# Positional terms of a block compression taken out of the data and added behind its first layer

## The chip, the cores and the metric

The kernel runs on one core of one Trainium2 chip. The metric is the device time of one execution in microseconds (us). The kernel before takes 863.8 us (median of three runs, 863.54 to 864.02).

## The reference, cut to what matters

One decoder layer over 512 tokens of width 1024: a norm and one wide input projection, two attention mixers (a sparse one called NSA with 8 heads in 2 groups, and a block one called MoBA with 8 heads), a gated merge with an output projection, a feed-forward block of width 2816, and a gated side input. The change touches one corner of NSA, the compression of keys and values. Every 32 neighbouring tokens (in steps of 16) become one flat row of 2048 numbers, a learned positional table `pe` is added, and a two-layer network makes one compressed key or value of 64 numbers from it:

```python
def compress_blocks(t, pe, w1, w2):
    b, g, sp, d = t.shape
    n_sub, per = sp // CMP_STRIDE, CMP_LEN // CMP_STRIDE      # 32 sub-blocks, 2 per block
    sub = t.reshape(b, g, n_sub, CMP_STRIDE, d)
    nc = n_sub - per + 1                                      # 31 blocks
    blocks = jnp.concatenate([sub[:, :, i:i + nc] for i in range(per)], axis=3)
    flat = (blocks + pe).reshape(b, g, nc, CMP_LEN * d)
    return jax.nn.silu(flat @ w1) @ w2

# in nsa_mixer
kc = rms_norm(compress_blocks(to_heads(kc_in, G), pe_k, ck_w1, ck_w2), kc_gain)
vc = compress_blocks(to_heads(vc_in, G), pe_v, cv_w1, cv_w2)
cmp_end = cmp_start + CMP_LEN - 1
s_c = jnp.einsum('bgrtd,bgcd->bgrtc', q, kc) * ATTN_SCALE
p_c = masked_softmax(s_c, cmp_end[None, :] <= t_idx[:, None])
o_c = jnp.einsum('bgrtc,bgcd->bgrtd', p_c.astype(vc.dtype), vc)
```

There are 31 blocks for each of the two groups. With two groups of 32 columns, columns 31 and 63 stand for no block; the mask takes them out of the softmax.

## The kernel before, in words

**Split products.** All large products are made in three passes of a rounded type (`F32R`): a number x is split into a high part h (a ScalarE copy that rounds) and a low part l = x - h (a VectorE subtraction), and TensorE adds h*h, h*l and l*h. This holds for the weights too. Every weight unit is loaded as `wr` (three buffers, issued on SP), split on ScalarE into `wh` (L84) and on VectorE into `wl` (L85), again with three buffers each. A raw buffer comes free, and its next load can start, when L85 has read it; a `wh` or `wl` buffer comes free when TensorE has used it.

**The stage in question.** The input projection of the MoBA queries (`qm`) comes first. Then come the compression's keys and values (`kvc`, tiles `kT` and `vT`, transposed: feature by token), the MoBA keys (`km`, four weight units) with the keys' first compression layer between them (`k1`, four units, in function `hidden`), then `cb`, `qn` with the values' first layer (`v1`), `cc`, `vm`, and after that attention, the gates, the output projection, the feed-forward block and the side input. Units are taken in the order km0, k1_0, km1, k1_1, km2, k1_2, km3, k1_3.

**`compress_in`** (L506 to L532), once for keys and once for values, evacuates the projected tile from PSUM with a factor (`kct`, L510), adds the positional table into a rearranged tile `x32` with eight additions of 64 partitions by 248 numbers (L520, half of them on VectorE, half on GpSimd; the source is read with a step of 16 numbers), and splits the result into high and low halves (L529 on ScalarE, L530 on VectorE, two 128x512 pieces each). These are the stationary operands of `hidden` (L580): one pass of 16 products with `wh` and 16 with `wl`, whose output rows 0 to 63 belong to the high part and rows 64 to 127 to the low one. `hidden` adds the two (L591, L593) and applies SiLU as z*(1+tanh(z/2)) (L594, L595), the factor one half being left to later. `cmp_kv` (L610) turns the 64x256 result with two TensorE transposes (L614), splits it (L617, L618), makes the second layer (L623, L624) and goes on to the compressed keys or values.

**Beside it** run the last steps of the `qm` heads: a rotation on GpSimd (L411 to L414), a split on ScalarE and VectorE (L419, L420, tile `qmst`), TensorE transposes (L439, tile `tb`) and their evictions on ScalarE (L446, tile `QM`).

**Order.** The kernel is written as interleaved generators, and a planner then orders the instructions of each engine: by the order of the program, among those that are ready in its own simulated time. Each engine runs its queue strictly in that order. Small work tiles (`t2`, 128x512) have five buffers, PSUM banks come in pairs by tag; `kT` and `vT` hold the two banks of tag `s`, which `km` needs for its first two token blocks.

Of the kernel before, what the change touches and what calls it, by code (L numbers as in the profile page):

```python
# [10 lines left out]
F32 = mybir.dt.float32  # L11
F32R = mybir.dt.float32r
I32 = mybir.dt.int32
AF = mybir.ActivationFunctionType
OP = mybir.AluOpType
# [7 lines left out]
DH = 64  # L23
# [143 lines left out]
def hybrid_kernel(ctx: ExitStack, tc: tile.TileContext, a, out):  # L167
    nc = tc.nc
    cp = ctx.enter_context(tc.tile_pool(name="cp", bufs=1))
# [5 lines left out]
    V, A, G, T = nc.vector, nc.scalar, nc.gpsimd, nc.tensor  # L175
# [13 lines left out]
    def t5(name, dt=F32):  # L189
        return pp.tile([128, 1280], dt, name=name, tag="t5")  # L190
# [75 lines left out]
    for tt in range(QT):  # L266
# [2 lines left out]

    hg = cp.tile([128, 6, DH], F32, name="hg")  # L270
    nc.sync.dma_start(hg, a["hg"].rearrange("(o h) d -> o h d", o=1).broadcast_to([128, 6, DH]))
    pe = cp.tile([128, 2, 2, 16], F32, name="pe")
    nc.sync.dma_start(pe, a["pe"])

    ident = cp.tile([128, 128], F32, name="ident")
    make_identity(nc, ident)
    identr = cp.tile([128, 128], F32R, name="identr")
    V.tensor_copy(identr, ident)
    half_neg = cp.tile([128, 32], F32, name="half_neg")
    V.memset(half_neg, -0.5)  # L280
    big_mask = cp.tile([128, 512], F32, name="big_mask")
# [2 lines left out]
                    channel_multiplier=1, compare_op=OP.is_ge, fill=BIG)  # L284
# [217 lines left out]
    qm_t, rest = norm_heads("qm", qm_b, None, q_tables[4])  # L502

    XX = {}

    def compress_in(i, nm):  # L506
        o = bank(nm + "T", "s")
        yield from ttile(("kvc", i), o)
        kt_ = t2("kct")
        V.scalar_tensor_tensor(kt_, o, 2.0, rb0, op0=OP.mult, op1=OP.mult)  # L510
        x32 = t5("x32")
        xv = x32[:, :1024].rearrange("p (j c) -> p j c", j=16)
        G.memset(xv[:, :, 31::32], 0.0)
        for g in range(2):
            gs = slice(64 * g, 64 * g + 64)
            kv = kt_[gs].rearrange("p (c j s) -> p s j c", s=2, j=8)
            for s in range(2):
                for hf in range(2):
                    eng = V if (g * 4 + s * 2 + hf) % 2 else G
                    eng.tensor_tensor(xv[64 * s:64 * s + 64, 8 * hf:8 * hf + 8, 32 * g:32 * g + 31],  # L520
                                      kv[:, s, :, hf:hf + 31],
                                      pe[gs, i, s, 8 * hf:8 * hf + 8].unsqueeze(2).to_broadcast([64, 8, 31]),
                                      op=OP.add)
        XX[nm] = []
        for hf in range(2):
            t = flat(t4(f"{nm}xx{hf}"))
            f = t.rearrange("p (j e c) -> p j e c", j=8, e=2)
            x = xv[:, 8 * hf:8 * hf + 8]
            A.activation(f[:, :, 0, :], x, AF.Copy)  # L529
            V.tensor_sub(f[:, :, 1, :], x, f[:, :, 0, :].bitcast(F32))  # L530
            XX[nm].append(t.rearrange("p (j c) -> p j c", j=8))
        yield  # L532

# [46 lines left out]
    def hidden(nm, tag):  # L580
# [10 lines left out]
        A.activation(tmp, o[64:128, :CH], AF.Copy)  # L591
        z = small("hz_", [64, CH])
        V.tensor_tensor(z, o[0:64, :CH], tmp, op=OP.add)  # L593
        A.activation(tmp, z, AF.Tanh, scale=0.5)  # L594
        V.scalar_tensor_tensor(z, tmp, 1.0, z, op0=OP.add, op1=OP.mult)  # L595
        hid[nm] = z

    KC = cp.tile([128, 2, 64], F32R, name="KC")
# [11 lines left out]
    def cmp_kv(i, nm, tag):  # L610
        b = bank(nm + "t2", tag)
        z = hid.pop(nm)
        for m in range(2):
            T.transpose(b[:, m * 64:(m + 1) * 64], z[:, m * 128:(m + 1) * 128], ident[0:64, 0:64])  # L614
        hs = MI[:, 512 + 256 * i:768 + 256 * i].rearrange("p (m e c) -> p m e c", m=2, e=2)
        bv = b[:, :128].rearrange("p (m c) -> p m c", m=2)
        A.activation(hs[:, :, 0, :], bv, AF.Copy, scale=0.5)  # L617
        V.scalar_tensor_tensor(hs[:, :, 1, :], bv, 0.5, hs[:, :, 0, :].bitcast(F32), op0=OP.mult, op1=OP.subtract)  # L618
        yield
# [430 lines left out]
def layout(i):  # L1050
# [20 lines left out]
    pos5 = np.concatenate([pos.reshape(QT, 128).T, np.tile(pos[cend], 4)[:, None]], axis=1)  # L1071

    def pet(p):
        t = p[0].reshape(16, 2, DH).transpose(2, 1, 0)
        return np.concatenate([t, t], axis=0)

    return dict(
        xT=f(i["x"][0].T.reshape(KT, 128, S)),
# [42 lines left out]
```

## Time and profile before

| | us |
|---|---|
| median of three runs | 863.8 |
| profiled execution, its own time | 863.29 |
| its span, first to last instruction | 861.4 |
| TensorE busy with products | 843.4 |
| VectorE busy | 532.2 |
| ScalarE busy | 391.3 |
| GpSimd busy | 139.2 |

The own time is the span and 1.9 us around it. Products overlap in the array, so TensorE shows as busy for a little longer than it issues; a stall costs the distance from one product's start to the next, less the usual distance. Times in the timelines are from the start of the span. A bracket at the end of a row is the engine's idle time ahead of that row and what ended it.

### The profile page before, as it was taken

The numbers are of one execution on the slowest core, as the hardware profiler recorded it, in microseconds if no ns is written. First come the engines' busy times: TensorE is split into PE (matmuls) and PEld (weight loads), VectorE is DVE, ScalarE is ACT, GpSimd is POOL, SyncE is SP. The second block draws the span as 40 slices with busy tenths as digits, with TensorE's granted clock in tenths as the row PEclk, the third lists the DMA queues.
The fourth block names the chain that finished last, engine by engine and source line by source line (L and its number), as shares of the span: only waits on it lengthen the run. The fifth ranks groups of instructions, "written<-read, shape, count | busy, mean of one in ns | idle before, by whom it ended". The sixth has DMA issues, their size and how long they took to land.

```text
span 861.4 us, 11012 instructions
## 1 busy us (share of the span) xinstructions
PE 843.4 (98%) x4169; PEld 708.5 (82%) x4169; DVE 532.2 (62%) x944; ACT 391.3 (45%) x708; POOL 139.2 (16%) x140
## 2 busy tenths in 40 slices
PE   9999999999999999999999999999999999999997
PEld 7878798888788888787888888888888888888886
DVE  6777766878976988749536555555555433233354
ACT  6455545877776877634423222233333222233421
POOL 2735443000000000024321111111111101010100
PEclk9999999999999999999999999999999999999999
DMA  9433525423211111116323333333323333333221
GB/s 328 153 99 98 162 73 142 129 64 89 84 49 50 50 49 36 63 49 216 102 76 121 98 98 97 99 98 97 95 91 94 84 109 87 93 110 97 98 99 49
DMA packets 26996, 85.58 MB, mean 99 GB/s; under 512 B 3392, under 2 KB 3904, under 8 KB 26944
## 3 DMA queue, kind: packets, MB, share of 16 engines
q1 hardware_dynamic: 26016, 82.78, 30.3%
q10 hardware_dynamic: 928, 2.11, 1.0%
q8 instruction: 32, 0.52, 0.3%
q14 instruction: 20, 0.16, 0.1%
HBM read 79.64 MB, written 2.10 MB: 95 GB/s over the span
## 4 chain that ended last, share of the span: by engine, by line
PE 84%; DVE 8%; ACT 2%; POOL 2%; DMA 2%; issue 1%; SPq 0%; DVEq 0%; ACTq 0%; POOLq 0%
PE fg L361 5%; PE fu L362 5%; PE fg L362 5%; PE fob L361 5%; PE fob L362 5%; PE fu L361 5%; PE fg L363 5%; PE fu L363 5%; PE fob L363 5%; PE ga L361 3%; PE ga L362 3%; PE ga L363 3%; PE pt L818 3%; DVE wl L85 2%; PE pgb L361 2%; PE pv L842 2%
## 5 line engine op out<-in xcount | busy, mean ns | idle before, releaser
L84 ACT ACTIVATE wh<-wr 128x1024 fp32r<-128x1024 f32 (+2 forms) x145 | 147.4, 1019 | 310.3 <-PE fu L362 73.6
L85 DVE TENSOR_TENSOR wl<-wr,wh 128x1024 fp32r<-128x1024 f32 (+2 forms) x145 | 196.2, 1357 | 106.0 <-ACT wh L84 105.4
L361 PE MATMUL fg<-x2h,wh 128*128 128x512 f32 x176 | 68.6, 390 | 0.0
L361 PE MATMUL fu<-x2h,wh 128*128 128x512 f32 x176 | 68.6, 390 | 0.0
L363 PE MATMUL fg<-x2h,wl 128*128 128x512 f32 x176 | 68.5, 389 | 0.0
L363 PE MATMUL fu<-x2h,wl 128*128 128x512 f32 x176 | 68.5, 389 | 0.0
L363 PE MATMUL fob<-HH,wl 128*128 128x512 f32 x176 | 68.5, 389 | 0.0
L362 PE MATMUL fu<-x2l,wh 128*128 128x512 f32 x176 | 68.5, 389 | 0.0
L362 PE MATMUL fg<-x2l,wh 128*128 128x512 f32 x176 | 68.5, 389 | 0.0
L362 PE MATMUL fob<-HL,wh 128*128 128x512 f32 x176 | 68.5, 389 | 0.0
L361 PE MATMUL fob<-HH,wh 128*128 128x512 f32 x176 | 68.5, 389 | 0.0
L1008 POOL TENSOR_TENSOR u<-zg,u 128x512 f32<-128x512 f32 x22 | 29.8, 1352 | 199.9 <-DVE u L1006 191.4
L361 PE MATMUL ga<-xh,wh 128*128 128x512 f32 x128 | 53.6, 419 | 0.0
L362 PE MATMUL ga<-xl,wh 128*128 128x512 f32 x128 | 50.3, 393 | 0.0
L363 PE MATMUL ga<-xh,wl 128*128 128x512 f32 x128 | 50.2, 393 | 0.0
L793 DVE CUSTOM_DVE_ANT_0 p<-sb,big_mask 128x512 f32<-128x512 f32 (+2 forms) x96 | 44.9, 484 | 7.3 <-PE sb L791 7.1
L1006 DVE SCALAR_TENSOR_TENSOR u<-fu,rb 128x512 f32<-128x512 f32 x22 | 15.2, 690 | 53.6 <-PE fu L363 53.6
L944 POOL TENSOR_TENSOR GT<-GT,GT 128x512 f32<-128x512 f32 x8 | 14.7, 1856 | 190.5 <-DVE GT L943 190.5
L245 POOL TENSOR_TENSOR ssum<-ssum,sqx 128x512 f32<-128x512 f32 x14 | 22.1, 1575 | 139.1 <-ACT sqx L244 139.1
L818 PE MATMUL pt<-ident,p 128*128 128x128 f32 x240 | 38.2, 274 | 2.8 <-DVE pw L828 2.7
L828 DVE TENSOR_TENSOR pw<-pt,pw 128x512 fp32r<-128x512 f32 x48 | 32.6, 684 | 10.7 <-ACT pw L827 10.3
L361 PEld LDWEIGHTS fu<-x2h,wh 128*128 128x128 f32 x176 | 33.1, 188 | 6.9
(590 smaller groups left out, 1993.5 us busy)
## 6 DMA issues: line engine op xcount, KB each, us to landing
wr<-fi SPq DMA_DIRECT2D x44, 512.0 KB, 3.4
wr<-ga SPq DMA_DIRECT2D x16, 512.0 KB, 3.5
wr<-fo SPq DMA_DIRECT2D x16, 512.0 KB, 3.5
wr<-wo SPq DMA_DIRECT2D x8, 512.0 KB, 3.6
wr<-pg SPq DMA_DIRECT2D x8, 512.0 KB, 3.4
wr<-fo SPq DMA_DIRECT2D x8, 384.0 KB, 3.2
xin<-xT SPq DMA_DIRECT2D x8, 256.0 KB, 5.5
xn<-xN SPq DMA_DIRECT2D x4, 512.0 KB, 7.8
```

The costliest lines, as they stand in the source:

```text
L84: self.nc.scalar.activation(h[:, a:b], t[:, a:b], AF.Copy)
L85: self.nc.vector.tensor_sub(l[:, a:b], t[:, a:b], h[:, a:b].bitcast(F32))
L245: G.tensor_tensor(ssum, ssum, q, op=OP.add)
L361: T.matmul(o, wh[:, sl], h, start=start, stop=False)
L362: T.matmul(o, wh[:, sl], l, start=False, stop=False)
L363: T.matmul(o, wl[:, sl], h, start=False, stop=stop)
L793: V.tensor_tensor_reduce(out=p, in0=o, in1=big_mask[:, 512 - n:512], op0=OP.add, op1=OP.min, scale=1.0, scalar=3.0e38, accum_out=st["m"][: ...
L818: last = T.transpose(b[:, off:off + 128], st["p"][:, P_OFF[qt] + kb * 128:P_OFF[qt] + kb * 128 + 128], ident)
L828: V.tensor_sub(pl, b[:, :off], ph.bitcast(F32))
L842: T.matmul(o, job["v"](kb), st.pop(("pl", kb))[:, cols], start=False, stop=job["last"] and kb == 2)
L1006: V.scalar_tensor_tensor(u, bu, 2.0, rb1, op0=OP.mult, op1=OP.mult)
L1008: G.tensor_tensor(u, zg, u, op=OP.mult)
```

## The change

The positional terms are no longer added to every block. The low-level layout of the table `pe` is changed so that it has the same rows as the rearranged operand, it is split once (`pes`), and its 16 columns for keys or values are put as one more block into the unused columns 31 and 63. The tile of projected keys (or values) is split before it is rearranged, once, and the high and low parts are then placed by copies: the high part on ScalarE, the low part on GpSimd. The first layer is linear, so the row of column 31 behind it is the positional contribution alone. It is added to all rows by the turn in `cmp_kv`: the two transposes become two products with `pos_sum`, an identity matrix whose row 31 is all ones. The nonlinearity has to come after this addition, so tanh and its multiplication move from `hidden` to `cmp_kv`, behind the turn.

```diff
-    pe = cp.tile([128, 2, 2, 16], F32, name="pe")
+    pe = cp.tile([128, 2, 16], F32, name="pe")
     nc.sync.dma_start(pe, a["pe"])
...
+    pos_sum = cp.tile([64, 64], F32, name="pos_sum")
+    V.tensor_copy(pos_sum, ident[0:64, 0:64])
+    G.affine_select(pos_sum, pos_sum, pattern=[[0, 64]], base=-31, channel_multiplier=1,
+                    compare_op=OP.not_equal, fill=1.0)
...
     XX = {}
+    pes = cp.tile([128, 2, 2, 16], F32R, name="pes")
+    A.activation(pes[:, 0], pe, AF.Copy)
+    V.tensor_sub(pes[:, 1], pe, pes[:, 0].bitcast(F32))
 
     def compress_in(i, nm):
         o = bank(nm + "T", "s")
         yield from ttile(("kvc", i), o)
         kt_ = t2("kct")
         V.scalar_tensor_tensor(kt_, o, 2.0, rb0, op0=OP.mult, op1=OP.mult)
-        x32 = t5("x32")
-        xv = x32[:, :1024].rearrange("p (j c) -> p j c", j=16)
-        G.memset(xv[:, :, 31::32], 0.0)
-        for g in range(2):
-            gs = slice(64 * g, 64 * g + 64)
-            kv = kt_[gs].rearrange("p (c j s) -> p s j c", s=2, j=8)
-            for s in range(2):
-                for hf in range(2):
-                    eng = V if (g * 4 + s * 2 + hf) % 2 else G
-                    eng.tensor_tensor(xv[64 * s:64 * s + 64, 8 * hf:8 * hf + 8, 32 * g:32 * g + 31],
-                                      kv[:, s, :, hf:hf + 31],
-                                      pe[gs, i, s, 8 * hf:8 * hf + 8].unsqueeze(2).to_broadcast([64, 8, 31]),
-                                      op=OP.add)
+        kh, kl = t2("kch", F32R), t2("kcl", F32R)
+        A.activation(kh, kt_, AF.Copy)
+        V.tensor_sub(kl, kt_, kh.bitcast(F32))
         XX[nm] = []
         for hf in range(2):
             t = flat(t4(f"{nm}xx{hf}"))
             f = t.rearrange("p (j e c) -> p j e c", j=8, e=2)
-            x = xv[:, 8 * hf:8 * hf + 8]
-            A.activation(f[:, :, 0, :], x, AF.Copy)
-            V.tensor_sub(f[:, :, 1, :], x, f[:, :, 0, :].bitcast(F32))
+            for e, src in ((0, kh), (1, kl)):
+                for g in range(2):
+                    kv = src[64 * g:64 * g + 64].bitcast(F32).rearrange("p (c j s) -> p s j c", s=2, j=8)
+                    for sh in range(2):
+                        o = f[64 * sh:64 * sh + 64, :, e, 32 * g:32 * g + 31]
+                        if e == 0:
+                            A.activation(o, kv[:, sh, :, hf:hf + 31], AF.Copy)
+                        else:
+                            G.tensor_copy(o, kv[:, sh, :, hf:hf + 31])
+                for c in (31, 63):
+                    G.tensor_copy(f[:, :, e, c:c + 1], pes[:, e, i, 8 * hf:8 * hf + 8].bitcast(F32).unsqueeze(2))
             XX[nm].append(t.rearrange("p (j c) -> p j c", j=8))
         yield
...
         V.tensor_tensor(z, o[0:64, :CH], tmp, op=OP.add)
-        A.activation(tmp, z, AF.Tanh, scale=0.5)
-        V.scalar_tensor_tensor(z, tmp, 1.0, z, op0=OP.add, op1=OP.mult)
         hid[nm] = z
...
         for m in range(2):
-            T.transpose(b[:, m * 64:(m + 1) * 64], z[:, m * 128:(m + 1) * 128], ident[0:64, 0:64])
+            T.matmul(b[:, m * 64:(m + 1) * 64], z[:, m * 128:(m + 1) * 128], pos_sum, start=True, stop=True)
+        th = t2("cth")[:, :128]
+        A.activation(th, b[:, :128], AF.Tanh, scale=0.5)
+        V.scalar_tensor_tensor(th, th, 1.0, b[:, :128], op0=OP.add, op1=OP.mult)
         hs = MI[:, 512 + 256 * i:768 + 256 * i].rearrange("p (m e c) -> p m e c", m=2, e=2)
-        bv = b[:, :128].rearrange("p (m c) -> p m c", m=2)
+        bv = th.rearrange("p (m c) -> p m c", m=2)
...
     def pet(p):
-        t = p[0].reshape(16, 2, DH).transpose(2, 1, 0)
-        return np.concatenate([t, t], axis=0)
+        return p[0].reshape(16, 2, DH).transpose(1, 2, 0).reshape(128, 16)
```

## Rows read from the trace of the kernel before

**Rows 1.** The page, part 1: busy us of TensorE, share, instructions.
```profile
PE 843.4 (98%) x4169; PEld 708.5 (82%) x4169; DVE 532.2 (62%) x944; ACT 391.3 (45%) x708; POOL 139.2 (16%) x140
```

**Rows 2.** Windows: stretch, its us, busy us of each engine, clock, DMA.
```profile
40.00:57.00 17.00, 14.86 (x79) 11.88 (x78) 16.46 (x21) 9.22 (x15) 10.64 (x12) 1.00 0.11 34
80.00:93.00 13.00, 9.83 (x58) 7.95 (x56) 11.14 (x12) 5.14 (x12) 10.94 (x9) 1.00 0.48 161
93.00:170.00 77.00, 75.80 (x443) 65.26 (x442) 54.48 (x117) 46.32 (x105) 21.65 (x25) 1.00 0.38 112
```

**Rows 3.** Timeline of TensorE, 44 to 57 us: start, us, what, [idle before].
```profile
44.30 0.94 PE L351 MATMUL km<-wh,xh 128*128 128x512 f32 x3
46.09 0.70 PE L439 MATMUL tb<-identr,qmst 128*128 128x128 f32 x6 [0.86 <-DVE qmst L420]
...
52.27 0.39 PE L351 MATMUL km<-wh,xh 128*128 128x512 f32 x1
52.49 0.39 PE L352 MATMUL km<-wl,xh 128*128 128x512 f32 x1
53.51 0.39 PE L586 MATMUL khid<-wh,kxx 128*128 128x256 f32 x1 [0.63 <-DVE kxx L530]
...
55.45 0.35 PE L586 MATMUL khid<-wh,kxx 128*128 128x256 f32 x1
56.45 0.39 PE L587 MATMUL khid<-wl,kxx 128*128 128x256 f32 x1 [0.65 <-DVE wl L85]
```

**Rows 4.** Timeline of VectorE, 41 to 59 us.
```profile
41.41 3.53 DVE L520 TENSOR_TENSOR x<-kct,pe 64x248 f32<-64x248 f32 x4
44.97 1.07 DVE L420 TENSOR_TENSOR qmst<-qme,qmst 128x512 fp32r<-128x512 f32 x1
...
47.69 3.83 DVE L520 TENSOR_TENSOR x<-kct,pe 64x248 f32<-64x248 f32 x4
...
52.77 1.29 DVE L530 TENSOR_TENSOR kxx<-x,kxx 128x512 fp32r<-128x512 f32 x2
...
55.18 3.58 DVE L85 TENSOR_TENSOR wl<-wr,wh 128x1024 fp32r<-128x1024 f32 x3
```

**Rows 5.** Timeline of ScalarE, 40 to 54 us.
```profile
40.92 1.05 ACT L84 ACTIVATE wh<-wr 128x1024 fp32r<-128x1024 f32 x1
46.67 1.16 ACT L419 ACTIVATE qmst<-qme 128x512 fp32r<-128x512 f32 x2 [4.71 <-POOL qme L414]
...
51.18 1.15 ACT L529 ACTIVATE vxx<-x 128x512 fp32r<-128x512 f32 x2 [2.32 <-POOL x L520]
52.24 1.06 ACT L446 ACTIVATE QM<-tb 128x512 fp32r<-128x512 f32 x2
53.20 1.06 ACT L84 ACTIVATE wh<-wr 128x1024 fp32r<-128x1024 f32 x1
```

**Rows 6.** Groups by line, shapes apart: count, busy us, mean ns, idle before.
```profile
L594 ACT ACTIVATE ht<-hz__1202 64x256 f32<-64x256 f32 x1 | 0.4, 404 | 0.0
L593 DVE TENSOR_TENSOR hz__775<-khid,ht 64x256 f32<-64x256 f32 x1 | 0.4, 408 | 0.0
L318 POOL COPY cs<-cs 128x40 f32<-128x40 f32 x1 | 0.2, 216 | 0.0
L594 ACT ACT_TABLE_LOAD x1 | 1.3, 1283 | 0.0
```

**Rows 7.** Timeline of GpSimd, 41 to 46 us.
```profile
41.77 3.71 POOL L520 TENSOR_TENSOR x<-kct,pe 64x248 f32<-64x248 f32 x4
45.56 1.08 POOL L414 TENSOR_TENSOR qme<-rope 128x256 f32<-128x256 f32 x1
```

**Rows 8.** The chain of work that ended last: start, us, engine, what.
```profile
106.27 0.27 PE kt L614 x2
457.15 0.89 PE st1c L336 x8
```

**Rows 9.** Timelines of ScalarE and TensorE, 102 to 112 us.
```profile
106.57 0.28 ACT L617 ACTIVATE MI<-kt 128x128 fp32r<-128x128 f32 x1 [2.97 <-PE kt L614]
...
111.20 0.27 PE L623 MATMUL ko<-MI 128*128 128x64 f32 x1
```

## The prediction

> **What bounds the kernel now.** I read the page's busy times first, then the windows by stage, then the timelines of the four engines in the one stage that the change touches.
>
> TensorE is busy for 843.4 us of a span of 861.4 [rows 1], so at most 18 us are to be had anywhere without taking products away, and the change takes none away. What matters is how much of that idle time lies where the compression runs. The windows [rows 2] answer it: from 40 to 57 us TensorE is busy for 14.86 of 17.00, and VectorE for 16.46 of 17.00. In this short stage VectorE is the bound and TensorE waits for it. From 93 to 170 us TensorE misses only 1.2 us.
>
> The timeline of TensorE [rows 3] shows three waits there, each ended by VectorE: for `qmst`, for `kxx`, for a `wl`. The usual distance between two products of 512 columns is 0.22 to 0.23 us (52.27 to 52.49), half of that for 256 columns. Against that, 44.30 to 46.09 holds three products (0.68) and loses 1.11 us; 52.49 to 53.51 loses 0.79; 55.45 to 56.45 loses 0.88. Together 2.8 us. Without them the product at 56.45 could start at 53.65.
>
> The timeline of VectorE [rows 4] shows why. Four additions of the positional terms hold it for 3.53 us from 41.41, and the subtraction for `qmst` follows only at 44.97; four more take 3.83 us from 47.69; then come four subtractions of the split (two pairs of 1.29) and only at 55.18 the weight's low part that TensorE wants at 56.45. ScalarE [rows 5] is held up behind this as well: it stands 2.32 us ahead of 51.18, waiting in order for the GpSimd additions of the values, and so rounds the weight k1_1 only at 53.20.
>
> **The change, part by part.**
>
> *VectorE.* Eight additions go: 3.53 + 3.83 = 7.4 us [rows 4]. Four 128x512 subtractions become two: at 1.29 a pair, 1.3 us less. What it gains is a 128x32 subtraction in the set-up, a copy of 64x64, and nothing else in this stage. So 8.7 us of 16.46 go, and VectorE is no longer the bound between 40 and 57 us. The subtraction for `qmst` at 44.97 moves ahead of 44.30, and the first stall goes. What is late next is ScalarE.
>
> *ScalarE.* Four roundings of 128x512 become two (1.15 us a pair [rows 5]); sixteen copies of 64x248 are added. The trace has no ScalarE copy with such a step between elements. From below, the nearest is the 64x256 activation at 0.404 us [rows 6], which read its source without a step; from above, a row of the same shape and step is the addition on VectorE, 3.53/4 = 0.88 us [rows 4], a different engine that shared its time with GpSimd. I take 0.40, the row of the same engine; both ends go into the range. Its queue after the rounding that ends at 41.97 [rows 5]: two roundings 1.15, sixteen copies 16c, the `qmst` pair 1.16, the `QM` pair 1.06, then k1_1's rounding 1.06. Copies of the values are not needed before 93 us, but stand ahead of k1_1 in the program, so I count all sixteen. The rounding ends at 41.97 + 4.43 + 16c = 46.4 + 16c, the subtraction for `wl` takes 1.2 us more (3.58 for three [rows 4]), and with 0.1 for the two hand-overs TensorE gets it at 47.7 + 16c. With c = 0.40 that is 54.1, against 56.45 before and 53.65 at the least: 2.35 us are won, 0.45 of the stalls stay. It breaks even at c = (56.45 - 47.7)/16 = 0.547.
>
> *GpSimd.* Eight additions go, 3.71 us for the first four [rows 7], and sixteen copies of 64x248 with sixteen of 128x8 come. From below, the copy of 128x40 takes 0.216 [rows 6]; from above, the addition took 3.71/4 = 0.93 [rows 7]. I take 0.6, between them, as a copy reads one operand and the additions waited for VectorE. TensorE needs first only the first half (4 large, 2 small for the low part, 2 small for the high part): from about 42.5, with the rotation of 1.08 ahead [rows 7], 42.5 + 1.08 + 4x0.6 + 4x0.2 = 46.8 at my value and 48.1 at the upper one. TensorE has km0 and km1 to do until about 51. So this is hidden, unless the order is unlucky (a rival below). The values' copies have until 93 us.
>
> VectorE's additions took 0.88 each beside GpSimd's and a 64x256 one alone takes 0.408 [rows 4, 6]. [...]
>
> *The turn and the nonlinearity.* In `hidden` a tanh (0.404) and a multiplication (0.41) leave, both beside `cb` products; nothing on TensorE waits. In `cmp_kv` a tanh and a multiplication of 128x128, some 0.3 each like the rounding of that shape (0.28 [rows 9]), enter between turn and second layer, with two hand-overs about 0.9 us. TensorE takes up the result only at 111.20, 4.6 us after ScalarE began at 106.57 [rows 9], so it is covered; without that cover it costs 0.9, twice. The table load of 1.28 us [rows 6] moves with the first tanh; ScalarE stands idle for 2.97 us ahead of 106.57 [rows 9], and the load does not wait for the turn, so it is covered; uncovered it costs 1.28. In ScalarE's queue behind the new tanh stand weight roundings; they are delayed by a third of a microsecond at most.
>
> *TensorE.* Four transposes become four full-precision products. Two transposes take 0.27, four 128x128 full-precision products 0.89 (eight records) [rows 8]: 0.13 against at most 0.22 each. That is 0 to 0.4 us in all, on the bounding engine; I take 0.2.
>
> *Set-up.* The split of `pe`, the 64x64 copy and selection: four small instructions before 40 us, where TensorE does not wait; nothing to 0.2 us. The load of `pe` stays one DMA on SP, smaller; weight loads keep their order and come earlier with the splits that free their buffers.
>
> **Sum.** 863.29 (span 861.4 and 1.9 around it) - 2.35 + 0.2 = 861.1 for a profiled execution. That execution lies 0.5 under the median of 863.8, so for the median 861.65, given as 861.6.
>
> **The rivals.**
>
> *The placing copies on ScalarE are dear (slower).* If a step of 16 numbers between elements costs ScalarE what it costs elsewhere, c is above 0.547 and k1_1 comes later than before. At c = 0.62 TensorE gets it at 57.6: 1.2 later, with 0.2 for the turn 865.2 by the median. At 0.76, not quite the upper end, at 59.9 and 867.4. For it: the additions with this step took twice a plain one; against it: they shared their time with GpSimd's, which alone would explain it. 0.14. [...]
>
> *The first layer is planned too early (no change).* The planner places `khid` as soon as it thinks `kxx` ready. If it believes the GpSimd copies to be quick, the products of k1_0 stand right behind km0, about 45.6, and TensorE waits in order until the low parts are there, 46.8 to 48.1 as worked out, say 1.4 later. Then 0.95 is won, less 0.2: 863.05. For it: the wait at 53.51 is already one for `kxx`; against it: TensorE had most of km1 done by then. 0.17.
>
> *The gain is given back between 57 and 93 us (no change).* From 80 to 93 us TensorE is busy for 9.83 of 13.00 [rows 2], waiting for weight splits on a VectorE that runs beside GpSimd. If those waits hang on something that does not move with TensorE, they grow by what was won: 863.8, or 864.0 with the turn. Against it: the chain there starts from the last `km` product, which moves too. 0.14.
>
> *More goes than I count.* If also some of the waits from 80 to 93 go, another 1 to 2 us: about 860. 0.05.
>
> **How the numbers follow.** The forecast has 0.50, with its own range 861.0 to 862.5 (from c = 0.372, where all 2.8 are won and the turn costs nothing, to c = 0.45). What this kernel can tell from no change is 0.2%, 1.7 us, so faster means below 862.1. About 0.42 of the forecast's 0.50 lies there, and the 0.05 of the last case: 0.47 faster. The other 0.08 of the forecast, the 0.17 of the second rival and 0.12 of the third: 0.37 same. The 0.14 of the first rival, and 0.02 of the third, where the waits grow by more than was won: 0.16 slower. The range for 8 in 10 reaches from 859.8 to 865.2, the upper end being c = 0.62.
>
> **What would show it.** In the changed profile between 40 and 57 us: VectorE busy for about 8 us instead of 16.5, TensorE missing under 1 us instead of 2.1, ScalarE busy for some 14. ScalarE's 64x248 copies at 0.40 and not 0.55; k1_1's `wh` beginning at 51 to 52 instead of 53.2. The table load at about 102 with nothing behind it. The forecast is wrong if `khid` waits for GpSimd, if ScalarE's copies are over 0.55, or if TensorE's idle time from 57 to 170 us grows.

## The result, and the profile after

The changed kernel takes 869.65 us (median of 6 runs, 868.57 to 870.69) against 863.83 us (6 runs, 862.30 to 866.51): a ratio of 1.0063, 95% interval 1.0049 to 1.0076. It is slower by 5.8 us, where 861.6 was forecast, and lies 4.45 us above the upper end of the range. Its profiled execution took 869.96 us, with a span of 868.1; that of the kernel before took 863.29, so the two profiles differ by 6.7 us.

The busy times, page part 1, against [rows 1]:

```profile
PE 848.4 (98%) x4173; PEld 712.6 (82%) x4173; DVE 524.4 (60%) x936; ACT 401.2 (46%) x723; POOL 146.4 (17%) x163
```

VectorE lost 7.8 us, as meant, and ScalarE gained 9.9. But TensorE, which has four products in place of four transposes and nothing else new, is busy for 5.0 us more. Such a figure cannot come from added work; it says that TensorE ran slower somewhere. The windows show where. Columns as in [rows 2]: stretch, its length, busy us of TensorE, of its weight loads, of VectorE, ScalarE, GpSimd, then the granted clock.

```profile
40.00:57.00 17.00, 13.91 (x71) 11.51 (x70) 8.28 (x9) 16.00 (x26) 16.27 (x35) 0.94 0.13 42
57.00:70.00 13.00, 12.46 (x55) 10.14 (x55) 4.97 (x4) 6.25 (x10) 2.09 (x3) 0.68 0.36 121
85.50:98.50 13.00, 9.84 (x58) 7.96 (x56) 11.14 (x13) 5.12 (x12) 10.94 (x9) 1.00 0.49 161
```

VectorE falls from 16.46 to 8.28 in the first stretch, which is the 8 us of the forecast. ScalarE stands at 16.00 of 17.00, and GpSimd, which got copies too, at 16.27; for which of them TensorE waits, the timelines tell. Behind this stretch, from 57 to 70, the granted clock is 0.68. The third line is the stretch of the second line of [rows 2], 5.5 us later: it has the same busy times.

The timeline of ScalarE, 44 to 59 us (start, busy us, what, and in brackets the idle time ahead of it), against [rows 5]:

```profile
43.34 1.16 ACT L423 ACTIVATE qmst<-qme 128x512 fp32r<-128x512 f32 x2 [0.52 <-POOL qme L418]
44.40 5.21 ACT L531 ACTIVATE kxx<-kch 64x248 fp32r<-64x248 f32 x8
49.63 0.63 ACT L519 ACTIVATE kch<-kct 128x512 fp32r<-128x512 f32 x1
50.30 5.14 ACT L531 ACTIVATE vxx<-kch 64x248 fp32r<-64x248 f32 x8
55.46 1.08 ACT L450 ACTIVATE QM<-tb 128x512 fp32r<-128x512 f32 x2
56.57 2.00 ACT L84 ACTIVATE wh<-wr 128x1024 fp32r<-128x1024 f32 x2
```

The sixteen placing copies (now L531) take 10.35 us, 0.65 each. Up to 59 us ScalarE is never idle again. The evictions of `QM` begin at 55.46, where they began at 52.24 before, and the weight of k1_1 is rounded from 56.57, where it was 53.20.

TensorE in the same time, against [rows 3]:

```profile
50.98 0.28 PE L591 MATMUL khid<-wh,kxx 128*128 128x256 f32 x1
...
52.63 0.40 PE L355 MATMUL km<-wh,xh 128*128 128x512 f32 x1
56.12 0.75 PE L443 MATMUL tb<-identr,qmst 128*128 128x128 f32 x4 [3.09 <-ACT QM L450]
...
59.19 0.58 PE L592 MATMUL khid<-wl,kxx 128*128 128x256 f32 x1 [0.54 <-DVE wl L85]
...
64.01 0.63 PE L355 MATMUL km<-wh,xh 128*128 128x512 f32 x1
64.43 0.63 PE L356 MATMUL km<-wl,xh 128*128 128x512 f32 x1
...
65.77 0.39 PE L355 MATMUL km<-wh,xh 128*128 128x512 f32 x1
66.00 0.40 PE L356 MATMUL km<-wl,xh 128*128 128x512 f32 x1
```

The wait for `kxx` at 53.51 of before is gone: `khid` starts at 50.98, and the wait ahead of `tb` at 46.09 is gone too. In their place stands one wait of 3.09 us for an eviction, and a shorter one for the weight. Then look at the distance between two products of 512 columns: 0.42 us at 64.01, and 0.23 again at 65.77. The windows of 2 us give the clock for it:

```profile
54.00:56.00 2.00, 0.00 (x0) 0.00 (x0) 0.00 (x0) 1.95 (x5) 1.85 (x4) 0.76 0.00 0
56.00:58.00 2.00, 1.89 (x10) 1.59 (x10) 0.34 (x1) 1.98 (x4) 1.87 (x4) 0.50 0.00 0
58.00:60.00 2.00, 1.46 (x7) 1.16 (x6) 2.00 (x2) 2.00 (x4) 1.13 (x2) 0.50 0.00 0
...
66.00:68.00 2.00, 2.00 (x13) 1.66 (x12) 0.00 (x0) 0.36 (x1) 0.00 (x0) 1.00 0.30 114
```

TensorE stood still from about 53 to 56.12. In that time its granted clock fell from 1.00 to 0.50, and it came back at about 65.3. At a granted clock of 0.50 a product of 512 columns takes 0.42 us in place of 0.23, which is where most of the 5.0 us of busy time come from.

The chain of waits from 54 to 61 us names the links in order: the last copies, the eviction, the rounding, the subtraction, the product.

```profile
54.81 0.63 ACT vxx L531
...
55.46 1.08 ACT QM L450 x2
...
56.57 1.06 ACT wh L84
...
57.66 1.49 DVE wl L85
...
59.19 0.58 PE khid L592
```

The turn, against the first line of [rows 8] (two transposes, next product 0.26 us after the first started, at 106.46 in that trace):

```profile
111.72 0.66 PE L617 MATMUL kt<-pos_sum,hz__811 64*128 64x64 f32 x4
112.31 0.53 PE L443 MATMUL tb<-identr,kmst 128*128 128x128 f32 x4
```

It takes 0.59 now, 0.33 more, and the other one the same.

### The profile page after: what moved, and what is told of

It reads as the page before. It is cut to its first block, busy times and chain, and to the rows that moved or that the text cites. A ratio compares the mean times of both kernels' runs of the same rounds, so it can differ in the third digit from the quotient of the medians.

```text
span 868.1 us, 11046 instructions
## 1 busy us (share of the span) xinstructions
PE 848.4 (98%) x4173; PEld 712.6 (82%) x4173; DVE 524.4 (60%) x936; ACT 401.2 (46%) x723; POOL 146.4 (17%) x163
## 4 chain that ended last, share of the span: by engine, by line
PE 85%; DVE 6%; ACT 2%; DMA 2%; POOL 2%; issue 1%; SPq 0%; DVEq 0%; POOLq 0%
PE fg L365 5%; PE fu L365 5%; PE fob L367 5%; PE fg L367 5%; PE fu L367 5%; PE fob L366 5%; PE fob L365 5%; PE fu L366 5%; PE fg L366 5%; PE ga L365 3%; PE ga L366 3%; PE ga L367 3%; PE pt L824 3%; DVE wl L85 2%; PE pgb L365 2%; PE pv L848 2%
## 5 line engine op out<-in xcount | busy, mean ns | idle before, releaser
L1014 POOL TENSOR_TENSOR u<-zg,u 128x512 f32<-128x512 f32 x22 | 29.8, 1353 | 199.9 <-DVE u L1012 191.4
L367 PE MATMUL ga<-xh,wl 128*128 128x512 f32 x128 | 50.2, 394 | 0.0
L367 PEld LDWEIGHTS fu<-x2h,wl 128*128 128x128 f32 x176 | 33.1, 188 | 6.9
```

Source lines behind the costliest of these rows:

```text
L367: T.matmul(o, wl[:, sl], h, start=False, stop=stop)
L1014: G.tensor_tensor(u, zg, u, op=OP.mult)
```

## The experiments

Each ratio is to the kernel before as timed beside that kernel, whose median there lay between 863.3 and 864.1; it is taken over all runs and can differ a little from the ratio of the two medians. The other columns are marks on TensorE's timeline in the profiles, us: the end of the wait in the `cb` products that stands at 81.97 before, and the first products of the first turn, of the scores `sb` and of the output projection `uno`.

| kernel | end of that wait | first turn | first `sb` | first `uno` | median, ratio to before [95%] |
|---|---|---|---|---|---|
| before | 81.97 | 106.20 | 156.43 | 366.6 | 863.83 |
| after | 87.50 | 111.72 | 163.03 | 373.1 | 869.65, 1.0063 [1.0049, 1.0076] |
| e1_plain | 80.36 | 104.6 | 155.9 | 365.9 | 863.08, 0.9994 [0.9985, 1.0003] |
| e2_later | 78.89 | 103.10 | 154.4 | 364.5 | 862.33, 0.9977 [0.9967, 0.9986] |
| e3_turn | 82.00 | 106.21 | 157.6 | 369.0 | 865.62, 1.0013 [1.0003, 1.0023] |
| e4_filled | 84.45 | 108.7 | 160.1 | 371.6 | 868.39, 1.0052 [1.0039, 1.0065] |
| e5_vector | 83.46 | 107.7 | 159.1 | 369.1 | 866.91, 1.0031 [1.0019, 1.0043] |
| e6_values_later | 80.71 | 104.9 | 155.2 | 365.4 | 863.35, 0.9990 [0.9980, 0.9999] |
| e7_plain_more | 84.45 | 108.7 | 160.0 | 370.0 | 867.58, 1.0040 [1.0026, 1.0054] |
| e9_later_turned | 78.67 | 102.92 | 153.9 | 364.8 | 861.58, 0.9982 [0.9974, 0.9991] |
| e10_reordered | 80.20 | 104.4 | 155.8 | 367.4 | 863.57, 1.0001 [0.9993, 1.0010] |
| e11_all | 78.90 | 103.1 | 154.1 | 365.0 | 861.66, 0.9981 [0.9972, 0.9990] |

The theory: ScalarE's copies are dear because their source steps by 16 numbers; by their time in ScalarE's queue they hold the evictions and the weight back; the wait that results lowers the clock; and the turn costs besides. The rivals: that number or place of the copies matters and not the step; that the clock falls for another reason; that the turn is most of it.

**e1_plain: the step taken away.** The ScalarE copies read 248 neighbouring numbers: as many, but not in the order that the result needs.

```diff
-    A.activation(o, kv[:, sh, :, hf:hf + 31], AF.Copy)
+    A.activation(o, src[64 * g:64 * g + 64, 0:248].bitcast(F32).rearrange("p (j c) -> p j c", j=8), AF.Copy)
```

> The changed kernel, but ScalarE's placing copies read 248 neighbouring numbers instead of every 16th (as many numbers, the same instructions and destinations; so the high parts are placed in a wrong order). Theory, the step between the numbers makes these copies dear: they take about 0.40 us instead of 0.65, the sixteen end 4 us sooner (about 51.5), the QM evictions behind them come before TensorE asks for their bank at 52.9, the 3.1 us wait and the half clock behind it go, total 861.5 to 863. Rival, it is the number of instructions on ScalarE and not the step: 0.65 us each, total 869.6.

863.08 us, 6.6 under the changed kernel (6.0 by the two ratios). The copies take 0.42 us, and the `QM` evictions begin at 51.20:

```profile
43.75 3.37 ACT L531 ACTIVATE kxx<-kch 64x248 fp32r<-64x248 f32 x8
...
47.81 3.37 ACT L531 ACTIVATE vxx<-kch 64x248 fp32r<-64x248 f32 x8
51.20 1.09 ACT L450 ACTIVATE QM<-tb 128x512 fp32r<-128x512 f32 x2
```

One wait is left between 50 and 60 us, for the weight's low part:

```profile
54.79 0.39 PE L592 MATMUL khid<-wl,kxx 128*128 128x256 f32 x1 [0.98 <-DVE wl L85]
```

Products of 512 columns stay 0.23 us apart behind it (59.55 to 59.78), and the granted clock of the whole profile is 0.999. So one number, 0.65 against 0.42, decides between 869.65 and 863.08. But the kernel is not faster than before by more than can be told, either: the price alone does not explain the forecast's miss.

**e2_later: the values' placing behind the km stage.** Same copies, same step; those of the values stand later in the order.

```diff
-        kh, kl = t2("kch", F32R), t2("kcl", F32R)
+        if nm == "v":
+            hl = t5("kchl", F32R)
+            kh, kl = hl[:, 0:512], hl[:, 512:1024]
+        else:
+            kh, kl = t2("kch", F32R), t2("kcl", F32R)
...
+        if nm == "v":
+            later.append(lambda: place(i, nm, kh, kl))
+        else:
+            place(i, nm, kh, kl)
...
+    later.pop()()
     km_t, rest = norm_heads("km", km_b, hg[:, 5])
```

> The changed kernel, but the copies that place the values are written behind the stage of the MoBA keys, so that the planner puts ScalarE's eight behind the QM evictions and the next weights (the split values wait in a larger tile). Theory, ScalarE's queue order delays the evictions: QM evictions at about 51, no wait of over 1 us between 50 and 58, clock 1.0 throughout, total 861.5 to 864. Rival, ScalarE has too much work wherever it stands: the wait comes back at the weights of km3 behind the copies and the total stays above 866.

862.33 us, ratio 0.9977: 0.2% faster than before. ScalarE has only the keys' eight copies ahead of the evictions, still at 0.65 us, and TensorE does not wait at all from 40 to 66 us:

```profile
40.00:57.00 17.00, 17.00 (x96) 14.44 (x95) 12.19 (x11) 16.07 (x26) 16.41 (x26) 1.00 0.26 82
57.00:66.00 9.00, 9.00 (x53) 7.62 (x52) 3.05 (x3) 8.22 (x14) 3.37 (x11) 1.00 0.35 101
```

The copies cost what they cost in the changed kernel, and ScalarE is as busy from 40 to 57 us; only what stands behind them differs. What the changed kernel loses is a place in the queue, not throughput.

**e3_turn: the new turn alone.** The kernel before, its additions kept, with the full-precision products and the nonlinearity behind the turn.

```diff
-            T.transpose(b[:, m * 64:(m + 1) * 64], z[:, m * 128:(m + 1) * 128], ident[0:64, 0:64])
+            T.matmul(b[:, m * 64:(m + 1) * 64], z[:, m * 128:(m + 1) * 128], pos_sum, start=True, stop=True)
```

> The kernel before with the new turn alone: pos_sum, products instead of transposes, tanh behind them. The positional terms are still added to each block, so the row that the turn adds is zero. Theory, the turn costs TensorE 0.3 us each (0.59 instead of 0.26 to the next product) and nothing else: 864.3 to 865.0. Rival one, it is covered: 863.8. Rival two, the later tanh delays the second layer and the scores: above 865.5.

Ratio 1.0013, 1.1 us; the median, 865.62, lies where the second rival has it (above 865.5), beside a kernel before that stood at 864.09. In the profile everything up to the turn is as before. From the first turn to the first `sb` product it takes 51.4 us instead of 50.2, but four transposes that the kernel before makes behind that product now stand ahead of it. The first product of the gates, `ga`, ahead of which both have made as many `sb` products and transposes, comes 55.7 us after the turn instead of 54.4 (161.87 and 160.63): 1.2 more. 0.66 of that are the products, twice 0.33. The rest are two short waits, one of 0.16 us ahead of 122.91 and this one, neither of which the kernel before has:

```profile
160.31 0.87 PE L443 MATMUL tb<-identr,kst 128*128 128x128 f32 x8 [0.40 <-DVE kc__1617 L633]
```

The changed kernel has both too, 0.16 at 128.42 and 0.41 at 165.78. So the theory that the products are all of it does not hold. That the waits come from the tanh and the multiplication behind the turn, as the second rival has it, was not shown. Further on, this profile shows 1.2 us more, from a second fall of the clock (last section).

**e4_filled: the wait filled with other products.** The changed kernel; 28 products of 256 columns, into columns that nobody reads, stand in TensorE's order ahead of the `tb` that waits.

```diff
+            if dst is QM and n == 2:
+                for _ in range(28):
+                    T.matmul(spare["k"][:, 256:512], xh[0][:, 0:128], xh[0][:, 0:256], start=False, stop=False)
```

> The changed kernel with 28 extra products of 256 columns (3.3 us, into unused columns of a bank) ahead of the transposes for which TensorE waits 3.1 us. They do nothing for the result and take no less time than the wait. Theory, about 4 us of the loss are the half clock that follows the wait: with TensorE kept at work the clock stays 1.0 and the total falls to about 865.5 though the eviction comes no sooner. Rival, the wait alone is the loss: 869.6 or more.

868.39 us, between the theory (865.5) and its rival (869.6). ScalarE's queue is the same, and the products that wait for it start at the same time (`khid` with `wl` at 58.79, 58.7 by the changed kernel less its 0.5 later start); what is left of the waits is 0.75 and 0.61. But the granted clock stays up:

```profile
52.00:56.00 4.00, 3.25 (x29) 3.05 (x27) 0.00 (x0) 3.93 (x7) 3.77 (x11) 1.00 0.00 0
56.00:58.00 2.00, 2.00 (x14) 1.67 (x13) 0.74 (x1) 1.98 (x3) 1.85 (x4) 1.00 0.00 0
```

The wait in the `cb` products ends at 84.45 instead of 87.50. Less the 0.5 of the start, 2.5 us of the changed kernel's loss in this stage are the clock's. The median shows only 1.3 of them; the profile has the second fall of the clock again: its `ga` products (from 164 us on) take up to 0.63 us, as in e3_turn, where those of the changed kernel take 0.50 at the most.

**e5_vector: the high parts placed by VectorE.**

```diff
-    A.activation(o, kv[:, sh, :, hf:hf + 31], AF.Copy)
+    V.tensor_copy(o, kv[:, sh, :, hf:hf + 31])
```

> The changed kernel with the sixteen placing copies of the high parts on VectorE, ScalarE has none of them. Theory A (ScalarE's queue is the cause: its 10.4 us of copies hold back the QM evictions and the weight's rounding, and the clock falls in the wait): the QM evictions begin near 46 to 50 instead of 55.46, no wait of 3 us ahead of the tb products, the granted clock stays at 1.00 between 52 and 66, median 862 to 864; what is left is decided by VectorE, which takes some 8 to 10 us of copies in place of the additions. Theory B (the placing by copies, whoever does it, or the turn is what costs): the copies delay the stage on VectorE as much, 868 or more. Step 16 on VectorE: 0.4 to 0.65 each beside GpSimd's copies.

866.91 us: better than on ScalarE, worse than forecast. The `QM` evictions begin at 44.51 and the 3.09 us wait is gone, as theory A has it. But now a weight's low part stands behind the copies in VectorE's queue:

```profile
43.26 4.86 DVE L531 CAST kxx<-kch 64x248 fp32r<-64x248 f32 x8
48.15 1.52 DVE L85 TENSOR_TENSOR wl<-wr,wh 128x1024 fp32r<-128x1024 f32 x1
```

```profile
49.72 0.50 PE L356 MATMUL km<-wl,xh 128*128 128x512 f32 x1 [2.58 <-DVE wl L85]
```

and the clock falls again, to 0.50 from 52 to 54 us. The cause has the same form on another engine: copies ahead of something that TensorE needs, then a wait, then half the clock.

**e6_values_later: before, with only the order changed.** The values' additions, rounding and split written behind the km stage, as in e2_later, but positional terms and turn as before.

```diff
+        if nm == "v":
+            later.append(lambda: place(i, nm, kt_))
...
+    later.pop()()
     km_t, rest = norm_heads("km", km_b, hg[:, 5])
```

> The kernel before, with the positional additions as they were, and only the values' share of them (additions, rounding, split) written behind the km stage. Theory A (the waits from 40 to 57 us come from values' work that stands too early in the order, and the gain of the run with the values placed later comes from that order alone): VectorE loses 3.83 + 1.29 us between 47 and 55, the waits at 53.51 and 56.45 shrink, median 861.5 to 862.5, as low or lower than the 862.33 of the changed kernel with its values placed later, since the turn costs nothing here. Theory B (the gain there came from taking the additions off VectorE): 863.5 to 864.

863.35 us, ratio 0.9990: between the two theories, nearer to B. The wait for `wl` is gone, that for `kxx` is there still, 0.79 us at 53.00. So the order alone is worth some 0.1%. Of the 3.1 us that e2_later gains up to the end of the `cb` wait (78.89 against 81.97) this kernel has 1.3 (80.71); by that difference the other 1.8 go with the rest of the change, of which the prediction named the additions taken off VectorE.

**e7_plain_more: plain copies, as much time.** As e1_plain, nine of the sixteen copies made twice.

```diff
+    for _ in range(2 if (g or (hf and sh and i)) else 1):
         A.activation(o, src[64 * g:64 * g + 64, 0:248].bitcast(F32).rearrange("p (j c) -> p j c", j=8), AF.Copy)
```

> The changed kernel with plain copies (source of 248 neighbouring numbers, so the high parts stand in another order), nine of the sixteen made twice: 25 x 0.42 = 10.5 us on ScalarE, as much as the sixteen copies with a step took (10.4). Theory A (only the time on ScalarE's queue counts): the wait of some 3 us ahead of the tb products is back, the granted clock falls to half after it, median 868.5 to 870. Theory B (a source with a step also disturbs other engines, or lowers the clock in another way): 863 to 865, clock at 1.00.

867.58 us, 4.5 above e1_plain. A was right that time in the queue suffices, without any step. It was wrong on the form: the planner put part of the values' copies behind the first evictions, and TensorE waits four times between 53 and 59 us, 0.50, 0.55, 1.14 and 0.63 us. The granted clock fell all the same:

```profile
58.00:60.00 2.00, 1.82 (x4) 1.50 (x5) 1.84 (x2) 2.00 (x5) 1.38 (x2) 0.54 0.43 166
60.00:62.00 2.00, 2.00 (x7) 1.60 (x6) 1.49 (x2) 0.99 (x2) 0.00 (x0) 0.60 0.82 262
```

**e8_steps and e12_step4: the price by itself.** Copies of 64x248 behind the last result of the kernel before, four of each kind; one line of e8_steps as a sample.

```diff
+    A.activation(oA.rearrange("p (j c) -> p j c", j=8), pa[0:64].rearrange("p (c j s) -> p s j c", s=2, j=8)[:, 0, :, 0:31], AF.Copy)
```

> The kernel before with a series of 64x248 copies behind its last result, engine after engine, the source stepping by 1, 2, 8 and 16 numbers, four of each, and at the end eight ScalarE copies of step 16 beside eight of GpSimd. Theory A (the step costs ScalarE, nothing else does): alone 0.42 at step 1 and 0.65 at step 16, rising at 2 and 8; beside GpSimd the same 0.65. Theory B (the 0.65 comes from sharing with GpSimd's copies): 0.42 at every step alone, 0.65 only beside GpSimd. VectorE alone: some 0.4 at step 1; GpSimd 0.6 to 0.7 alone. The whole time is some 35 us above the kernel before, and only the durations are read.

> The kernel before with copies of 64x248 behind its last result, engine after engine, four of each: a source that steps by 4 numbers, and a plain source with a result that steps by 16. Theory A (a copy is dear when neighbouring elements lie more than a few numbers apart in the source): ScalarE and GpSimd at step 4 between the 0.45 of step 2 and the 0.67 of step 8, and the stepped result costs nothing, 0.42 on ScalarE. Theory B (reads and writes with a step cost alike): 0.6 or more for the stepped result too. VectorE's first pass of 128x512 with a stepped result took 1.13 against 0.68, which speaks for theory B there. Only the durations are read.

ScalarE of e8_steps, source stepping by 2, 8 and 16 numbers, and last by 16 again while GpSimd makes copies of its own (with steps of 1, 2 and 8 in that time):

```profile
858.03 1.79 ACT L1055 ACTIVATE prx<-pra 64x248 fp32r<-64x248 f32 x4
859.86 2.69 ACT L1057 ACTIVATE prx<-pra 64x248 fp32r<-64x248 f32 x4
862.58 2.57 ACT L1059 ACTIVATE prx<-pra 64x248 fp32r<-64x248 f32 x4
867.21 5.22 ACT L1080 ACTIVATE prx<-prb 64x248 fp32r<-64x248 f32 x8 [2.06 <-POOL prb L1078]
```

ScalarE of e12_step4, a plain source and a result stepping by 16:

```profile
860.26 2.60 ACT L1055 ACTIVATE prx<-pra 64x248 fp32r<-64x248 f32 x4
```

Time of one copy, in us:

| step | ScalarE | VectorE | GpSimd |
|---|---|---|---|
| source 1 | 0.41 | 0.31 | 0.43 |
| source 2 | 0.45 | 0.31 | 0.45 |
| source 4 | 0.65 | 0.40 | 0.66 |
| source 8 | 0.67 | 0.40 | 0.67 |
| source 16 | 0.64 | 0.38 to 0.42 | 0.64 |
| result 16 | 0.65 | 0.61 | 0.64 |

The price is ScalarE's own: 0.64 alone, 0.65 beside GpSimd. Theory B of e8_steps, that sharing makes it, falls. It jumps between a step of 2 and one of 4 numbers, from 0.45 to 0.65, and stays there (0.67 at 8, 0.64 at 16), and on ScalarE and GpSimd a result with a step of 16 costs the same (0.65 and 0.64), so theory B of e12_step4 holds for them. VectorE's 0.61 was taken while GpSimd copied beside it; how much of it is the step stays open. For 248 elements on ScalarE a step of 4 costs 0.24 us, 0.65 against 0.41. Why the time jumps just there was not shown.

**e9_later_turned: e2_later with the transposes back.** The positional column is added behind the turn.

```diff
-            T.matmul(b[:, m * 64:(m + 1) * 64], z[:, m * 128:(m + 1) * 128], pos_sum, start=True, stop=True)
+            T.transpose(b[:, m * 64:(m + 1) * 64], z[:, m * 128:(m + 1) * 128], ident[0:64, 0:64])
+        u = t2("cu")[:, :128]
+        for m in range(2):
+            V.tensor_scalar(u[:, m * 64:(m + 1) * 64], b[:, m * 64:(m + 1) * 64], b[:, m * 64 + 31:m * 64 + 32], None,
+                            op0=OP.add)
...
```

> The changed kernel with its values placed later (as in the run of that name), and the turn made by the transposes of the kernel before; the positional terms are added to the turned block by two VectorE additions of 128x64 with a number per partition. Theory A (the full-precision products cost 0.33 a turn on TensorE, and nothing behind them hides it): 0.26 instead of 0.59 from the turn to the next product, twice, so 0.7 under the 862.33 with the values placed later: 861.6. Theory B (the additions and the tanh come on the path in their place, as nothing covers some 0.8 more): 862.5 to 863.5. In both the ratio to the kernel before is under 0.998.

861.58 us, but by its ratio (0.9982 against 0.9977) no better than e2_later: the kernel before stood lower beside it, at 863.29 against 864.09. Between the turn and the next product are 0.26 us again, and the first `sb` comes 0.5 earlier than in e2_later (0.2 of that is there at the turn already), yet `uno` 0.3 later. Neither theory is confirmed; the 0.7 us did not come back in full.

**e10_reordered: the step moved to one pass.** VectorE's first pass writes its result in the order in which the copies read.

```diff
-        V.scalar_tensor_tensor(kt_, o, 2.0, rb0, op0=OP.mult, op1=OP.mult)
+        V.scalar_tensor_tensor(kt_.rearrange("p (q c) -> p c q", q=16), o.rearrange("p (c q) -> p c q", q=16), 2.0,
+                               rb0.rearrange("p (c q) -> p c q", q=16), op0=OP.mult, op1=OP.mult)
...
-    kv = src[64 * g:64 * g + 64].bitcast(F32).rearrange("p (c j s) -> p s j c", s=2, j=8)
+    kv = src[64 * g:64 * g + 64].bitcast(F32).rearrange("p (j s c) -> p s j c", s=2, j=8)
```

> The changed kernel with one edit: VectorE's first pass over the compressed rows writes them in the order in which the copies read, so that the copies on ScalarE and GpSimd read runs of 31 neighbouring numbers. Theory A (the step in the source is the cause): ScalarE's copies at 0.42 and not 0.65, GpSimd's cheaper too, QM evictions at about 51.3, no wait of 3 us, clock at 1.00 from 40 to 70, median 862.5 to 863.5, as in the run with plain copies, less the 0.3 that a pass with a step costs more on VectorE. Theory B (the number or the shape of the copies is the cause, and the plain run gained by something else): 867 or more.

863.57 us, 6.1 under the changed kernel (5.4 by the ratios), with every number in its right place: the step is the cause of the loss, and theory B falls. GpSimd's copies read neighbouring numbers here too; e1_plain changes ScalarE's alone and gains as much. The granted clock is 1.00 from 40 to 70 us, and one wait is left there, 0.88 us for the weight's low part at 54.61. VectorE pays 0.45 a pass (1.13 instead of 0.68), ScalarE gets the copies at 0.41:

```profile
39.06 1.13 DVE L517 SCALAR_TENSOR_TENSOR kct<-kT,rb 128x512 f32<-128x512 f32 x1
```

```profile
43.68 3.36 ACT L532 ACTIVATE kxx<-kch 64x248 fp32r<-64x248 f32 x8
47.73 3.37 ACT L532 ACTIVATE vxx<-kch 64x248 fp32r<-64x248 f32 x8
51.12 1.09 ACT L450 ACTIVATE QM<-tb 128x512 fp32r<-128x512 f32 x2
```

**e11_all: the edits of e2_later, e9_later_turned and e10_reordered together.**

> All three edits together: values placed later, rows written in the order of the copies, the turn by transposes with the positional terms added behind it. Theory A (after the values are out of the way TensorE has no wait left from 40 to 70 us, so cheaper copies bring nothing more): the same as the run with later values and transposes, 861.6. Theory B (the copies still cost through VectorE and GpSimd, which keep later weight splits back): 0.5 to 1 lower, about 861.

861.66 us, ratio 0.9981, as e9_later_turned: once TensorE does not wait in this stage, cheaper copies bring nothing, as theory A has it.

## Why the prediction was wrong

It named the right stage, the right engine to watch and the right rival, and gave that rival 0.14.

*The step that failed: "I take 0.40, the row of the same engine."* That row had no step in its source, and the text said so. The copies cost 0.65, over the break-even of 0.547 that the prediction had worked out itself. In the sum of the execution, 16 times 0.25 is 4.0 us. The formula itself was only a little low. At c = 0.65 it has TensorE get the weight at 58.1; it was 59.19, or 58.6 without the 0.6 us by which all products of this profile start later. With plain copies (e1_plain, c = 0.42) it has 54.4, and it was 54.79. Some 0.3 of this is the subtraction for `wl`, 1.49 us where 1.2 was counted. GpSimd's copies ran beside it, and the last of them, of a shape that takes 0.19 at the median, took 1.08 and ended with it:

```profile
58.11 1.08 POOL L535 CAST vxx<-pes 128x8 fp32r<-128x8 f32 x1
```

In e5_vector three such subtractions beside GpSimd's copies take 4.66 us (from 56.30, 1.55 each), and the next, at 62.40 with GpSimd idle, takes 1.22. The prediction's sum has nothing for this.

The bound from above, 0.88 from VectorE, was set aside since GpSimd shared its time. VectorE alone takes 0.4 for a copy of that shape and step, 0.1 more than for a plain one, so the step can be only a small part of that row; but ScalarE pays 0.24 for it. The text says that both ends go into the range, yet the range stops at c = 0.62. With 0.88 the formula gives 869.3, nearly the measured time; that would have been luck, as the copies cost 0.65 and the clock, which the formula leaves out, made up for the rest.

*A step that was missing: the clock.* The first rival was priced as lateness alone, 865.2 at c = 0.62; at the measured 0.65 the same sum gives 865.65, just outside the range. The wait it makes also took the clock, 2.5 us by e4_filled, and that takes the time far out of the range. The windows of before [rows 2] show 1.00 for waits of about 1 us each; no row of before had one of 3 us.

*A step with the wrong link.* The prediction followed the weight to `khid`. The first to be late were the evictions of `QM` that stand ahead of it in ScalarE's queue: 3.09 us for them, 0.54 for the weight. Both ends are nearly the same time; the order decides where TensorE stands still.

*The turn: "0 to 0.4 us in all; I take 0.2."* It was 1.2 up to the first `ga` product: twice 0.33 for the products, whose bound from above (0.22 each) came from 128x128 products and was too low for these, and 0.57 in the two short waits up to 166 us. The prediction had looked at the pick-up of the first turn at 111.20 [rows 9] and no further. So even with plain copies (e1_plain, e10_reordered) nothing is left that can be told from no change: 1.6 to 1.8 us won in the stage, 1.2 lost at the turn.

The sum then, from profile to profile, 6.7 us: 0.6 is start-up scatter (first `kT` product at 29.8 instead of 29.2; the other runs have 29.0 to 29.3). From there to the end of the wait in `cb`, 87.50 against 81.97, 4.9 more. From there to the first turn nothing (24.2 in both). From the first turn to the first `ga`, 1.2. The 4.9 of the stage are the forecast's -2.35, the 4.0 of the copies, the 2.5 of the clock, and 0.75 that remain, of which about 0.5 is the weight's coming later than the formula has it. That split rests on e4_filled's one profile.

*What was right.* VectorE's relief (8.28 left of 16.46), the first `khid` product no longer late, and GpSimd's copies hidden. Their size was off: the large ones of the keys took 0.6 to 1.5 us each, where 0.6 was taken and 0.93 was the upper end.

```profile
43.98 4.24 POOL L533 CAST kxx<-kcl 64x248 fp32r<-64x248 f32 x4
```

With the small ones behind these four, the first half was placed at about 48.6, past the 48.1 worked out for the upper end. But TensorE came to `khid` only at 50.98 and did not wait for them, so the second rival did not happen. The third did not either: the waits of 80 to 93 us recur 5.5 us later at their old size (0.96 against 0.95, 1.41 against 1.42). The table load moved to 109.14, and ScalarE stands idle behind it until the turn:

```profile
109.14 1.28 ACT L619 ACT_TABLE_LOAD   x1
112.41 0.28 ACT L619 ACTIVATE cth<-kt 128x128 f32<-128x128 f32 x1 [1.99 <-PE kt L617]
```

Of the forecast of 2.35 us in the stage, e2_later has 3.1, with the same dear copies, once the values stand behind what TensorE needs; but 1.3 of that is the new order alone, by e6_values_later, which the forecast did not have.

What stays open: which of its small waits keep e9_later_turned from the 0.7 us of the transposes, and why the second fall of the clock comes in some profiles and not in others.

## What to carry to other kernels

A copy that changes the order of elements is priced by its access pattern: a row of the same engine without the step is a lower bound, not an estimate (on ScalarE 0.41 us without, 0.65 with it), and where the break-even lies between the bounds the chance belongs in the middle. Work that is moved to an idle engine takes a place in its queue; ask first what TensorE needs from behind it, and put what is not needed soon after that, which here was worth more (ratio 0.9977) than copies at 0.42 in place of 0.65 (0.9994). A new wait on TensorE is to be priced with the clock that may fall in it, as after the 3.09 us here, when 2.5 us went with it (e4_filled).

## What was not expected of the hardware

After 3.09 us in which TensorE stood still, its granted clock was 0.50 for some 9 us, though it was busy for most of them; after four waits of 2.8 us in all between 53 and 59 us (e7_plain_more) it was 0.54 and 0.60 for 4 us.

The same happens, in some executions, at a wait that the kernel before has as well: 1.45 us for `pw`, at about 234 us. In the profile of before the clock stays at 1.00 there; in that of e3_turn, with the same 1.45 us ahead of 235.63, it falls and costs 1.2 us (the first line has the wait):

```profile
234.00:236.00 2.00, 0.55 (x5) 0.44 (x4) 2.00 (x6) 1.69 (x6) 0.00 (x0) 0.82 0.00 0
236.00:238.00 2.00, 2.00 (x7) 1.61 (x6) 1.79 (x8) 1.50 (x6) 0.00 (x0) 0.50 0.00 0
```

It stands in the profiles of e4_filled (`ga` products of up to 0.63 us) and e10_reordered (0.83 from 232 to 242 us) too. The scatter of 2 to 4 us between runs of one kernel fits this. Of 27 runs of the kernel before, the 15 with a mean granted clock of 0.998 took 864.95 us on average, the 9 with 1.00 863.46; ten of the eleven runs of e3_turn (865.62 on average) and all five of e4_filled have 0.998. So part of e3_turn's loss can be a clock that falls more often: among runs at 0.998 it is 0.7 us. The mean does not tell where the clock fell (in the profile of e11_all, 0.998 too, no `ga` product takes over 0.50 us), so that the scatter is this wait was not shown. GpSimd and ScalarE have nearly the same price for these copies, at every step (0.43 and 0.41, 0.64 and 0.64).
